# Attention by two pairs of heads at a time, and the order tables that go with it

## The chip, the cores and the metric

The kernel runs on one core of one Trainium2 chip. The metric is device time in microseconds (us) of one execution, lower is better. Engines are named as in the profile: PE (TensorE matmuls) and PEld (its weight loads), DVE (VectorE), ACT (ScalarE), POOL (GpSimd) and SP (SyncE, which issues most of the loads).

## What is computed

Two decoder layers over 256 tokens of width 1024. Layer 0 mixes tokens by a gated MLP, layer 1 by causal attention of 12 heads of 64; beside either stands a 4-head cross-attention into 256 memory tokens, and behind it an output projection, a LayerNorm of `alpha*x + sub`, a SwiGLU of inner width 2816 and another LayerNorm. Cut to what matters here:

```python
for i in range(2):
    if i == 0:
        u, v, q_mem = jnp.split(x @ a_w_in, ...)
        # gelu, LayerNorm of v; per group g: u * (tril(w_s[g]) @ v + b_s[g])
        mix = gmlp_mixer(u, v, ...)
    else:
        q, k, v, q_mem = jnp.split(x @ b_w_in, ...)
        # 12 heads of 64; the sequence is one block, so this is plain causal attention
        mix = moba_attention(q, k, v)
    mem_out = memory_cross_attention(q_mem, mem, w_mem_kv[i])     # 4 heads
    sub = jnp.concatenate([mix, mem_out], axis=-1) @ w_mix_out[i]
    x = layer_norm(ALPHA * x + sub, ...)
    x = layer_norm(ALPHA * x + swiglu(x, w_ffn_in[i], w_ffn_out[i]), ...)
```

## The kernel before, in words

Nearly every product is made from operands split into a high and a low part (`split`, L378: ACT rounds the high part, DVE subtracts it to get the low one), with three passes: high by high, low by high, high by low. Weights stream from memory in units of up to 1 MB (SP issues them, four buffers), and each half unit is split by ACT and DVE into one of ten buffers ahead of PE's use (`Stream`). PSUM holds eight tiles of 128 by 512: four with the tag acc (`acc_tile`, L382) and four with the tag mm (`mm_tile`, L385). A tile's bank comes free when its last reader is done.

**What sets the order.** PE executes its instructions in the order in which `build` writes them. DVE, ACT and SP execute theirs in the order of three tables (L293, L324, L349): number n is the n-th instruction that `build` gives to that engine, and `keep_order` (L358) forces the sequence. All engines run in order, so an instruction that waits holds back whatever its table places behind it. POOL has no table; it computes the reciprocal roots of the normalisations, masks the position weights wsT, and adds some weight blocks by DMA.

**Layer 0 around the change (L943 to L995).** On PE follow each other: the u projections (pu), the memory keys (hkm, from `mem_k`), the position products (sv, L968), the first half of the memory values (pvm, `mem_v`, L620), the memory scores (sm, `mem_scores`, L585), the second half of the memory values, and the output projection (opa). The position products multiply vn (the normalised v, made by DVE) as a 128-row, 64-column operand by wsT, three tiles of two groups of channels each. DVE then adds the bias (the third tile's bias is a load of its own, `in_bs`), multiplies by u, and splits the outcome into the mix tiles that the output projection reads.

**Layer 1's attention (L1041 to L1126).** Heads go in pairs, hp = 0 to 5. For one pair:

- `qk_half(hp, j)` (L1044): the projection to queries (j = 0) or keys (j = 1), 16 matmuls of the full array (qk in the profile); the result is split into the tile qks.
- `scores(hp)` (L1054): 12 matmuls that contract over 64 rows, the pair's two heads in the two halves of the array's rows (s), followed by a `Softmax` for each head (L557): DVE adds the mask and finds the row's extreme in a narrow (128) and a wide (256) part, ACT takes the two exponentials with their sums (z), and `normalise` on DVE takes the reciprocal and multiplies the two parts.
- `att_t(hp)` (L1063): six transposes (pt), copied to pT by ACT.
- `att_pv(hp)` (L1074): the value products, eight matmuls into 64 columns, one half of the columns for each head (pv); ACT and DVE split the result into mix[hp].

The memory attention of layer 1 does the same with its own scores (sm), transposes (ptm, `mem_transposes`, L597) and value products (pvm, `mem_pv`, L610, also 64 columns). In the old loop over i, pair i's projection halves alternate with the transposes of pair i-2, the scores of pair i-1 and the value products of pair i-2; every score group and nearly every value group stands alone between full-width products. The second halves of the projections use acc tiles, the first halves mm tiles.

The output projection (`OutProj`, L687) adds one term of six matmuls for each mix tile k and each of two token tiles tt (`step`, opc in the profile); `close` ends a token tile with its last two terms, followed by the LayerNorm's sums on DVE, the reciprocal root on POOL, the offset on DVE (ofc) and the scaling of two halves on ACT (L525). Then PE transposes the token tile (ptc, L531) for the FFN.

Of the kernel before, what the change touches and what calls it, by code (L numbers as in the profile page):

```python
# [21 lines left out]
P = 128  # L22
D = 1024
T = 256
# [169 lines left out]
class Stream:  # L194
# [128 lines left out]
)  # L323
SCALAR_ORDER = (  # L324
# [23 lines left out]
)  # L348
SYNC_ORDER = (  # L349
# [5 lines left out]
)  # L355


def keep_order(nc, tc, engine, order):  # L358

    mine = [i for i in nc.cur_bb.bb.instructions if i.engine == engine and not str(i.opcode).startswith("Tile")]  # L360
    assert len(mine) == len(order), (engine, len(mine))
    for a, b in zip(order, order[1:]):
        tc.add_manual_dep(mine[b], mine[a].name, mybir.DependencyInfo(
# [3 lines left out]
def build(nc, tc, ins, out):  # L367
    ET = mybir.EngineType
    with (
# [714 lines left out]
        for i in range(6):  # L1084
# [4 lines left out]
            if i >= 2:  # L1089
                pTs[i - 2] = att_t(i - 2)  # L1090
# [121 lines left out]
```

## Time and profile before

| what | value |
|---|---|
| median of 3 runs | 556.6 us (555.95 to 556.95) |
| the profiled execution's own time | 555.88 us |
| its span, first to last instruction | 554.1 us |
| mean granted TensorE clock | 0.997 |
| PE busy | 545.3 us, 98% of the span |
| PEld busy | 459.0 us, 83% |
| DVE busy | 501.9 us, 91% |
| ACT busy | 372.5 us, 67% |
| POOL busy | 49.5 us, 9% |
| moved by DMA | 120.97 MB, mean 218 GB/s |

The profile is of one execution. Rows of the chain of waits read "start, length, engine, tile, source line, count": the chain is followed back from the last instruction to whatever released each step. All matmuls carry L404, the line of a helper, so tiles tell them apart; 's' are scores, 'pv' value products, 'sv' position products. Rows of a timeline add the operation, the operands and, in brackets, how long the engine stood idle before and who ended that. A timeline's durations overlap a little from one instruction to the next. Rows of the stages give, for a stretch of time, the busy time and number of instructions of PE, PEld, DVE, ACT and POOL, the granted clock, the DMA share and GB/s.

### The profile page before, as it was taken

The numbers are of one execution on the slowest core, as the hardware profiler recorded it, in microseconds if no ns is written. First come the engines' busy times: TensorE is split into PE (matmuls) and PEld (weight loads), VectorE is DVE, ScalarE is ACT, GpSimd is POOL, SyncE is SP. The second block draws the span as 40 slices with busy tenths as digits, with TensorE's granted clock in tenths as the row PEclk, the third lists the DMA queues.
The fourth block names the chain that finished last, engine by engine and source line by source line (L and its number), as shares of the span: only waits on it lengthen the run. The fifth ranks groups of instructions, "written<-read, shape, count | busy, mean of one in ns | idle before, by whom it ended". The sixth has DMA issues, their size and how long they took to land.

```text
span 554.1 us, 7689 instructions
## 1 busy us (share of the span) xinstructions
PE 545.3 (98%) x2835; PEld 459.0 (83%) x2835; DVE 501.9 (91%) x707; ACT 372.5 (67%) x573; POOL 49.5 (9%) x59
## 2 busy tenths in 40 slices
PE   8999999999999999999999999999999999999994
PEld 8988878888888888888898888788888888888884
DVE  4799968999999999999989876578999999999997
ACT  4777768776768777773656767568767786877540
POOL 1002003020202010100100000101202020201001
PEclk9999999999999999999999999999999999999998
DMA  8997289467897788787368441172598798897622
GB/s 291 390 401 268 91 318 281 153 100 227 235 331 173 228 281 246 249 287 271 118 246 340 158 161 72 26 249 105 89 302 179 248 271 287 228 271 216 189 78 76
DMA packets 23718, 120.97 MB, mean 218 GB/s; under 512 B 2688, under 2 KB 4736, under 8 KB 13824
## 3 DMA queue, kind: packets, MB, share of 16 engines
q1 hardware_dynamic: 17344, 99.16, 47.5%
q0 software_dynamic: 5760, 20.97, 21.2%
q10 hardware_dynamic: 576, 0.34, 0.3%
q8 instruction: 22, 0.36, 0.3%
q14 instruction: 16, 0.13, 0.1%
HBM read 119.42 MB, written 1.05 MB: 217 GB/s over the span
## 4 chain that ended last, share of the span: by engine, by line
PE 96%; DMA 2%; SPq 1%; DVE 1%; issue 0%; ACT 0%; DVEq 0%
PE fof L404 11%; PE Xg L404 10%; PE Xf L404 10%; PE fog L404 9%; PE Zf L404 7%; PE Zg L404 7%; PE qk L404 6%; PE opc L404 4%; PE opa L404 4%; PE bv L404 3%; PE pu L404 3%; PE pvm L404 3%; PE hkm L404 2%; PE hqm L404 2%; PE pg L404 2%; PE pf L404 2%
## 5 line engine op out<-in xcount | busy, mean ns | idle before, releaser
L379 ACT CAST spl_s_M<-raw_s_T 128x1024 fp32r<-128x1024 f32 x80 | 82.8, 1053 | 35.9 <-DVE raw_s_T L259 32.1
L380 DVE TENSOR_TENSOR spl_s_M<-raw_s_T,spl_s_M 128x1024 fp32r<-128x1024 f32 x80 | 96.4, 1219 | 1.7 <-ACT spl_s_M L379 1.5
L379 ACT CAST spl_s_M<-raw_s 128x1024 fp32r<-128x1024 f32 x60 | 61.1, 1052 | 18.8 <-DMA raw_s<-in_w 13.9
L380 DVE TENSOR_TENSOR spl_s_M<-raw_s,spl_s_M 128x1024 fp32r<-128x1024 f32 x60 | 72.1, 1219 | 0.9 <-ACT spl_s_M L379 0.8
L404 PE MATMUL fof<-spl_w,htf 128*128 128x512 f32 x264 | 63.0, 390 | 0.0
L404 PEld LDWEIGHTS fof<-spl_w,htf 128*128 128x128 f32 x264 | 49.3, 188 | 10.2
L404 PE MATMUL fog<-spl_w,htg 128*128 128x512 f32 x228 | 54.2, 390 | 0.0
L380 DVE TENSOR_TENSOR spl_w<-raw_w,spl_w 128x1024 fp32r<-128x1024 f32 x44 | 53.1, 1219 | 0.8 <-ACT spl_w L379 0.8
L404 PEld LDWEIGHTS fog<-spl_w,htg 128*128 128x128 f32 x228 | 42.7, 188 | 8.8
L259 DVE TENSOR_TENSOR raw_s_T<-raw_s_T,raw_s 128x1024 f32<-128x1024 f32 x40 | 48.6, 1219 | 0.3
L379 ACT CAST spl_w<-raw_w 128x1024 fp32r<-128x1024 f32 x44 | 45.3, 1053 | 0.0
L220 POOL DMA_DIRECT2D raw_s<-in_w x20 | 17.2, 858 | 222.8 <-DVE spl_s_M L380 164.8
L404 PE MATMUL qk<-x2T,spl_qk 128*128 128x512 f32 x192 | 36.6, 344 | 0.0
L404 PEld LDWEIGHTS qk<-x2T,spl_qk 128*128 128x128 f32 x192 | 29.3, 188 | 5.2 <-issue 0.6
L404 PE MATMUL Xf<-spl_s_M,SfM 128*128 128x512 f32 x120 | 29.4, 393 | 0.0
L404 PE MATMUL Xg<-spl_s_M,SgM 128*128 128x512 f32 x120 | 29.3, 393 | 0.0
L404 PE MATMUL Xg<-spl_s_M,x3T 128*128 128x512 f32 x120 | 29.1, 390 | 0.0
L404 PE MATMUL Xf<-spl_s_M,x1T 128*128 128x512 f32 x120 | 29.0, 390 | 0.0
L404 PE MATMUL Zf<-spl_s_M,SfM 128*128 128x512 f32 x120 | 28.9, 389 | 0.0
L404 PE MATMUL Zg<-spl_s_M,SgM 128*128 128x512 f32 x120 | 28.8, 389 | 0.0
L404 PEld LDWEIGHTS Xg<-spl_s_M,x3T 128*128 128x128 f32 x120 | 22.4, 188 | 5.2 <-DVE x3T L380 0.4
L404 PEld LDWEIGHTS Xf<-spl_s_M,x1T 128*128 128x128 f32 x120 | 22.4, 188 | 4.9 <-DVE m5f L805 0.3
(264 smaller groups left out, 1070.5 us busy)
## 6 DMA issues: line engine op xcount, KB each, us to landing
raw_w<-in_w SPq DMA_DIRECT2D x22, 1024.0 KB, 6.9
raw_s<-in_w SPq DMA_DIRECT2D x20, 1024.0 KB, 7.0
raw_s_T<-in_w SPq DMA_DIRECT2D x10, 1024.0 KB, 6.0
raw_s_T<-in_w POOLq DMA_DIRECT2D x20, 512.0 KB, 7.9
raw_s<-in_w POOLq DMA_DIRECT2D x20, 512.0 KB, 5.6
raw_o<-in_w SPq DMA_DIRECT2D x8, 1024.0 KB, 7.2
raw_qk<-in_w SPq DMA_DIRECT2D x6, 1024.0 KB, 4.8
raw_v<-in_w SPq DMA_DIRECT2D x7, 512.0 KB, 8.7
```

What stands on the lines that cost most here:

```text
L220: self.nc.gpsimd.dma_start(self.raw[name][:, sl], self.unit_ap(other)[:, sl], accum_op=ALU.add)
L259: self.nc.vector.tensor_add(raw, raw, self.raw[used[1]][:, sl])
L379: nc.scalar.copy(hi, src)
L380: nc.vector.tensor_sub(lo, src, hi.bitcast(F32))
L404: nc.tensor.matmul(o, lhsT, rhs, start=start, stop=stop, skip_group_check=on)
```

## The change

The work is the same; its order changes. In layer 0 the first half of the memory values goes ahead of the position products, which so come directly before the memory scores. In layer 1 the loop over single pairs is written out for groups of two pairs: `pair_scores` makes the scores of two pairs and normalises their four softmaxes, `values` makes the value products of two pairs directly ahead of the next group's scores, and the memory value products (`mem_pv`) stand directly ahead of the scores of pairs 0 and 1. Both projection halves now use mm tiles, scores take acc tiles except those of pair 5, which take mm tiles. At the end, the output terms 0, 1 and 2 of token tile 0 stand in one run, the transposes of pairs 4 and 5 follow each other, and the term (1, 7) stands ahead of the closing of token tile 0. The three order tables are new throughout. Cut to its core:

```diff
@@ SCALAR_ORDER (start)
-    2, 0, 3, 4, 5, 6, 7, 9, 8, 11, 12, 10, 13, 14, 15, 17, 18, 16, 19, 26, 22, 27, 1, 24, 20, 31, 23, 32, 25, 41, 42,
+    2, 3, 4, 5, 6, 7, 8, 9, 11, 10, 13, 14, 12, 15, 16, 0, 17, 1, 18, 19, 26, 27, 22, 24, 25, 31, 20, 32, 23, 41, 21,
...
@@ SYNC_ORDER (start)
-    0, 1, 2, 3, 4, 18, 5, 6, 7, 8, 9, 11, 10, 12, 13, 14, 19, 20, 16, 21, 15, 17, 24, 25, 23, 22, 26, 27, 28, 29, 32,
+    0, 1, 2, 3, 4, 18, 5, 6, 7, 8, 10, 9, 11, 12, 13, 14, 15, 19, 20, 16, 17, 24, 22, 25, 21, 26, 27, 28, 29, 23, 31,
...
@@ layer 0
+        vm_part = mem_v("vm0", memx)
+        vm = vm_part(0)
         for jj in range(3):
             sv = acc_tile(f"sv{jj}").rearrange("p (j c t) -> p j c t", j=2, c=2)
...
-        vm_part = mem_v("vm0", memx)
-        vm = vm_part(0)
         nc.scalar.preload_act_table(AF.Exp)
         pr = mem_scores(qm, km, "m0", (acc_tile, acc_tile, mm_tile, mm_tile))
...
@@ layer 1
         def qk_half(hp, j):
-            t = (acc_tile if j else mm_tile)(f"qk{hp}{j}")
+            t = mm_tile(f"qk{hp}{j}")
...
-        def scores(hp):
+        def scores(hp, tile):
             st = qks[hp]
-            ss = [acc_tile(f"s{hp}{par}") for par in range(2)]
+            ss = [tile(f"s{hp}{par}") for par in range(2)]
...
+        def pair_scores(hps, tiles):
+            for n, hp in enumerate(hps):
+                prs[hp] = scores(hp, tiles[n])
+            for hp in hps:
+                for p in prs[hp]:
+                    p.normalise()
+
+        def values(hps):
+            for hp in hps:
+                att_pv(hp)
+
+        qk_half(0, 0)
+        pr_mem = mem_scores(qm, km1, "m1", (acc_tile, acc_tile, mm_tile, mm_tile))
+        qk_half(0, 1)
...
+        for p in pr_mem:
+            p.normalise()
+        qk_half(1, 0)
+        pts = mem_transposes(pr_mem, "1", (0, 1))
+        qk_half(1, 1)
+        pts += mem_transposes(pr_mem, "1", (2, 3))
+        qk_half(2, 0)
+        mem_pv(pts, vm1, mix, "1")
+        pair_scores((0, 1), (acc_tile, acc_tile))
+        qk_half(2, 1)
+        qk_half(3, 0)
+        pTs[0] = att_t(0)
+        qk_half(3, 1)
+        pTs[1] = att_t(1)
+        qk_half(4, 0)
+        values((0, 1))
+        pair_scores((2, 3), (acc_tile, acc_tile))
+        qk_half(4, 1)
+        qk_half(5, 0)
+        pTs[2] = att_t(2)
+        qk_half(5, 1)
+        pTs[3] = att_t(3)
         op = OutProj(1, mix, "c")
         op.step(0, [6, 7], first=True)
+        values((2, 3))
+        pair_scores((4, 5), (acc_tile, mm_tile))
+        op.step(0, [0, 1, 2])
         pTs[4] = att_t(4)
-        prs[5] = scores(5)
-        for p in prs[5]:
-            p.normalise()
-        op.step(0, [0])
-        att_pv(4)
-        op.step(0, [1])
         pTs[5] = att_t(5)
-        op.step(0, [2])
-        att_pv(5)
+        op.step(0, [3])
         op.step(1, [6], first=True)
-        op.step(0, [3])
+        values((4, 5))
+        op.step(1, [7])
         op.close(0, [4, 5], xres)
-        op.step(1, [7, 0, 1, 2, 3])
+        op.step(1, [0, 1, 2, 3])
```

Read through `build`, the table entries that the prediction speaks of mean this. On ACT, 10 and 12 are the copies of the fifth and sixth x0T (0 is the first table load, 17 the last value cast). On SP, 29 is the load of raw_km1 and 23 that of the third bias. On DVE, the softmaxes of pairs 4 and 5 stand at the places 447 to 468 of the new table, with the low halves of mix 2 and 3 among them, and in front of them the two halves of the first FFN weight and the last three steps of qks5.

More of the change, by code (lines that the diff above doesn't have):

```diff
@@ L1081, in att_pv @@
             split(mix[hp][:, 0, :], mix[hp][:, 1, :], o[:, :256])
-        pts = []
-        for i in range(6):
-            qk_half(i, 0)
-            if i in (1, 2):
-                for p in pr_mem[2 * i - 2:2 * i]:
-                    p.normalise()
-            if i >= 2:
-                pTs[i - 2] = att_t(i - 2)
-            if i >= 1:
-                prs[i - 1] = scores(i - 1)
-                for p in prs[i - 1]:
-                    p.normalise()
-            if i == 0:
-                pr_mem = mem_scores(qm, km1, "m1", (acc_tile, acc_tile, mm_tile, mm_tile))
-            qk_half(i, 1)
-            if i == 0:
-                mix += [actp.tile([P, 2, T], F32R, tag=f"mix{k}", name=f"mix1_{k}") for k in range(6, KT)]
-            if i >= 2:
-                att_pv(i - 2)
-            if i in (1, 2):
-                pts += mem_transposes(pr_mem, "1", (2 * i - 2, 2 * i - 1))
-            if i == 3:
-                mem_pv(pts, vm1, mix, "1")
+        def pair_scores(hps, tiles):
[3 more added lines that the diff above has]
+                for p in prs[hp]:
+                    p.normalise()
@@ new lines, in values @@
+        def values(hps):
[4 more added lines that the diff above has]
+        qk_half(0, 1)
+        mix += [actp.tile([P, 2, T], F32R, tag=f"mix{k}", name=f"mix1_{k}") for k in range(6, KT)]
+        for p in pr_mem:
[4 more added lines that the diff above has]
+        pts += mem_transposes(pr_mem, "1", (2, 3))
@@ L1108, in build @@
+        pair_scores((4, 5), (acc_tile, mm_tile))
+        op.step(0, [0, 1, 2])
         pTs[4] = att_t(4)
-        prs[5] = scores(5)
-        for p in prs[5]:
-            p.normalise()
-        op.step(0, [0])
-        att_pv(4)
-        op.step(0, [1])
         pTs[5] = att_t(5)
-        op.step(0, [2])
-        att_pv(5)
+        op.step(0, [3])
         op.step(1, [6], first=True)
-        op.step(0, [3])
+        values((4, 5))
+        op.step(1, [7])
         op.close(0, [4, 5], xres)
-        op.step(1, [7, 0, 1, 2, 3])
+        op.step(1, [0, 1, 2, 3])
```

110 rows, old and new, of tables (SCALAR_ORDER, SYNC_ORDER, VECTOR_ORDER) are left out of this document.

## The prediction

> **What bounds the kernel now.** I read the page first, then the busy time by stage, then the chain of waits in order of time, then the timelines of DVE and ACT around the attention of layer 1.
>
> ```profile
> span 554.1 us, 7689 instructions
> ...
> PE 96%; DMA 2%; SPq 1%; DVE 1%; issue 0%; ACT 0%; DVEq 0%
> ```
>
> The chain that ends last is PE for 96% of the span. So a microsecond counts only if PE's own sequence gets shorter, or if PE is made to wait. The next view gives busy time by stage (columns PE, PEld, DVE, ACT, POOL, clock, DMA share, GB/s).
>
> ```profile
> 51.00:61.50 10.50, 10.50 (x106) 9.24 (x106) 10.50 (x20) 7.41 (x14) 0.00 (x0) 1.00 0.42 130
> 298.43:370.34 71.91, 71.91 (x474) 58.53 (x475) 53.37 (x157) 47.93 (x120) 2.30 (x3) 1.00 0.44 148
> 447.00:478.00 31.00, 31.00 (x143) 25.70 (x142) 29.90 (x30) 22.48 (x27) 4.29 (x5) 1.00 0.89 263
> ```
>
> PE has no gap in any of them. In the attention stretch (second row) DVE has 18.5 us to spare and ACT 24, so small additions there hide. In layer 0's gating (first row) DVE has nothing to spare: what comes late there comes late for good. In the FFN (third row) the change moves nothing but orders, and I cost that at nothing: the DVE fills 29.9 of 31.0 us and follows PE, which releases its buffers; were that cover gone, each microsecond of DVE delay would show as one.
>
> A PE that is always busy can still lose time, and the chain shows where (start, length, what):
>
> ```profile
> 51.04 2.77 PE sv L404 x48
> 53.81 3.03 PE pvm L404 x16
> ...
> 61.47 6.83 PE opa L404 x30
> ...
> 71.44 1.88 PE pvm L404 x16
> ...
> 306.79 3.02 PE qk L404 x16
> ...
> 310.67 2.78 PE qk L404 x16
> ...
> 327.21 0.81 PE pv L404 x8
> 328.01 1.73 PE pvm L404 x16
> 329.74 3.03 PE qk L404 x16
> ...
> 357.83 12.51 PE opc L404 x54
> ```
>
> The same 16 products of a projection half take 2.78 us behind transposes (310.67), but 3.02 behind scores (306.79) and 3.03 behind value products (329.74). The memory value products take 1.88 behind full-width products and 1.73 straight behind pv, which has their shape (128 rows by 64 columns). So each passage between the full array and a part of it costs something, and products of one shape side by side pay nothing between them. **Prices:** leaving scores 3.02-2.78 = 0.24; leaving value products 0.25; entering value products 1.88-1.73 = 0.15. Entering scores has no row of its own: bounds are 0 and 0.24, the price of leaving them, and I take 0.15, the entry of the other part shape. One visit to scores then costs 0.39, one to values 0.40.
>
> **The change part by part.**
>
> *Visits in layer 1.* The scores of the memory attention keep their place. Besides them the old order makes six visits for scores and six for values (pv1 and pvm stand together): 6 x 0.39 + 6 x 0.40 = 4.74 us. The new one makes four: pvm with scores 0 and 1, values 0 and 1 with scores 2 and 3, values 2 and 3 with scores 4 and 5, values 4 and 5 alone. Three of them enter as values and leave as scores (0.15 + 0.24), one is of values (0.40): 1.57 us, and three boundaries inside, from 128x64 values to 64x128 scores, which no row shows. Below, such a boundary could cost 0, as between pv and pvm; above, all of a leaving and an entering, 0.40. I take 0.2, because both sides are parts but not the same part, and the nearest row, an entry of 0.15, is a change of shape too. Saved: 4.74 - 1.57 - 0.6 = 2.57 (1.97 to 3.17).
>
> [...]
>
> *The visit in layer 0.* The position products (sv) now stand directly before the memory scores, and the first half of the memory values, a full-width product, goes ahead of them. Two visits (0.40 + 0.39) become one with a boundary inside (0.15 + 0.24 + 0.2): 0.2 saved (0 to 0.4, by the boundary's bounds). All else on PE is the same products in another order.
>
> *The start.* The new ACT table puts the fifth x0T copy ahead of the sixth, and moves the first table load (it ran while ACT waited for data) in front of the last value cast.
>
> ```profile
> 13.81 0.71 ACT L439 CAST x0T<-raw_v 128x256 fp32r<-128x256 f32 x2 [0.43 <-DMA raw_v<-in_w]
> ```
>
> ACT waited 0.43 us for the sixth copy's data with the fifth queued behind it, and PE's products of the fifth step began after it. I credit 0.2 (0 to 0.43). The table load is hidden by the four steps of products that PE still has ahead of it there; without that cover its whole length would show.
>
> *Softmaxes four at a time.* This is what the change adds as a wait. Behind scores 4 and 5 PE has only the terms 0, 1, 2 of the output projection, 18 x 0.23 = 4.1 us (54 products in 12.51 above; a term is six), where two softmaxes stood before and four stand now. On ACT and DVE one softmax is made of these (the second fence is DVE):
>
> ```profile
> 352.28 0.51 ACT L576 ACTIVATE pb<-pb,mb 128x256 f32<-128x256 f32 x1 [0.34 <-DVE mb L567]
> 352.69 0.19 ACT L576 ACTIVATION_READ_ACCUMULATOR pb<-pb,mb 128x1 f32 x1
> 352.79 0.39 ACT L576 ACTIVATE pb<-pb,mb 128x128 f32<-128x128 f32 x1
> ...
> 353.67 0.35 ACT L379 CAST mix<-pv 128x256 fp32r<-128x256 f32 x1
> ...
> 368.91 0.81 ACT L525 ACTIVATE xres<-xres,ofc,rsc 128x512 f32<-128x512 f32 x1
> ```
>
> ```profile
> 350.62 0.42 DVE L380 TENSOR_TENSOR mix<-pv,mix 128x256 fp32r<-128x256 f32 x1 [2.59 <-ACT mix L379]
> ...
> 353.79 0.17 DVE L580 RECIPROCAL zb<-zb 128x2 f32<-128x2 f32 x1
> 353.99 0.55 DVE L582 TENSOR_SCALAR pb<-pb,zb 128x256 f32<-128x256 f32 x2
> ...
> 366.17 0.16 DVE L523 SCALAR_TENSOR_TENSOR ofc<-mvc,rsc 128x1 f32<-128x1 f32 x1 [0.74 <-POOL rsc L522]
> ```
>
> A wide exponential holds ACT for 0.51, a narrow one for 0.39, and a mix copy takes 0.35; neighbours overlap by 0.09 or so (352.69 + 0.19 against 352.79). Count from the first output term after the scores. Scores 4 end about one score earlier, so ACT's first exponential can begin at -0.3 (estimate). In the new ACT table the wide one of pair 4's second head is the seventh entry: three narrow, two wide and two mix copies, 2.9 less 0.2 of overlap, end at 2.4. DVE then has a reciprocal (0.17), two normalisings (0.55 the pair) and the low half of pair 2's values (0.42), 1.1: done at 3.5. PE wants that half a third into its third term, at 0.1 + 14 x 0.23 = 3.3. I reckon 0.2 us of waiting here. By the same count DVE's last normalising ends at 5.1, and its transposes stand at 5.0: 0.1. Before all this, score 5 starts as DVE finishes the last low half of qks5, which now stands behind two weight halves: 0.2. The earlier groups have two projection halves, 5.8 us, before their first transposes and four softmaxes are 4 x 0.9 on ACT, so nothing. Together 0.5 (0 to 1.5).
>
> *Ends that move closer.* The term (1, 7) moves ahead of the closing of tile 0, so that 24 products instead of 30 cover tile 0's normalisation. That closing now ends 24 products into the last 54, at 357.8 + 24 x 0.23 = 363.4, and the offset is there at 366.3 (the 366.17 row): 2.9 us, plus two scalings of 0.81 (the 368.91 row): 4.5, under 24 x 0.23 = 5.5. The new ACT table lets both scalings follow each other, where a weight cast stood between them. Nothing, with 1.0 in hand; were it gone, each microsecond would show. The j=1 halves move from the acc to the mm banks: their readers are done before the next tile asks, except for score 5, counted above. The memory softmaxes are normalised before the second projection group instead of across two: DVE has the slack.
>
> *Position products later.* sv needs both normalised vn halves, and memory value half 0 gives DVE 3.0 us more for them, of which the new DVE table spends most on output weights put ahead. I take 0.15 of waiting (0 to 0.8).
>
> **Sum:** 2.57 + 0.2 + 0.2 - 0.5 - 0.15 = 2.3 us. Against the profiled execution, 555.88 us (span 554.1 and 1.8 around it), this gives 553.6; that execution lies 0.7 under the median of the runs, 556.6, so the median to expect is 554.3. Not all bounds are met at once; with the boundary at either end and half of the others the case runs from 553.2 to 555.7.
>
> **The rivals.**
>
> *More is saved.* The boundary inside a visit costs nothing: 4 x 0.2 more, 553.5. For it: pv and pvm. Against it: the shapes differ here.
>
> *The softmaxes come late everywhere.* Each of the three groups in layer 1 waits about 0.6 more than reckoned, 1.7 together: 556.0, no change that can be told (0.2%, 1.1 us, is about what a measurement of this kernel can tell). For it: ACT and DVE are in fixed order, and casts that wait for weight buffers stand among the exponentials. Against it: DVE's slack.
>
> *Nothing is saved.* The price hangs on each group of products and not on the passage: 2.77 less, 557.1, within what can't be told. Against it: 1.73 beside 1.88.
>
> *Slower, through a bias.* The load of the third group's bias moves, in SP's queue, behind a weight load that waits for a free buffer.
>
> ```profile
> raw_km<-in_w SPq DMA_DIRECT2D x1, 1024.0 KB, 5.0
> ...
> vn<-in_bs SPq DMA_DIRECT2D x1, 128.0 KB, 10.0
> ```
>
> ```profile
> 51.54 0.33 SPq L241 DMA_DIRECT2D raw_km<-in_w  x1
> ```
>
> If that weight load is issued at 51.5 as before, the bias follows at 52 and lands behind its 5.0 us, at 57, just when the third bias add wants it (sv ends at 51.04 + 3.03 + 2.77 = 56.8 now). If it takes 10.0 us as before, it lands at 62, and DVE, in order, holds the mix halves, the memory softmaxes and the second half of output weight 0 behind that add. By my count of the new DVE table that weight half is split one microsecond before PE wants it for its second output term (61.5 + 1.4 = 62.9); 5 us later on DVE are 4.0 lost on PE: 558.3. It turns to a loss from a landing at about 60.3. Against it: the 10.0 was with other loads ahead of it, and around 52 the core moves only 130 GB/s (first row of the stages).
>
> **How the numbers follow.** Forecast 0.60, more saved 0.10, late softmaxes 0.18, nothing saved 0.03, the bias 0.09. The first two are faster: 0.70; the next two about the same: 0.21; the last slower: 0.09. The range is the forecast's own, opened downward for a cheaper boundary and a better start at once, and upward for the late softmaxes: 552.9 to 556.4.
>
> **What would show it.** In the chain after: projection halves at 3.0 us only behind scores, three in the main stretch and not ten; scores in pieces of about 1.6 for two pairs; values in pieces of 1.5; output terms without a break. Wrong on the boundary: a pair of scores behind values beginning with no gap, or with 0.4. Wrong on the softmaxes: PE waiting at the third output term, or before pt, for DVE. Wrong on the bias: gt's third add idle on a DMA. PE starting earlier than 14.58 would confirm the start; a wait at sv, the last term.

## The result and the profile after

| | before | after | ratio, 95% interval |
|---|---|---|---|
| first comparison, medians of 5 runs | 556.6 us (555.68 to 556.95) | 552.6 us (552.34 to 553.36) | 0.9933 [0.9919, 0.9948] |
| second comparison (run a2 below) | 555.89 us (11 runs) | 552.72 us (5 runs) | 0.9948 [0.9936, 0.9960] |
| the profiled execution | 555.88 us, span 554.1 | 552.48 us, span 550.8 | |

The change is faster by 3.7 us (2.9 to 4.5) in the first comparison and by 2.9 us (2.2 to 3.6) in the second. The prediction was 554.3 us, with a range from 552.9 on. The direction was right, the size was not: 552.6 lies just below that range.

From the page of the kernel after (span; PE's row; the shares of the chain that ended last):

```profile
span 550.8 us, 7698 instructions
...
PE 542.6 (99%) x2835; PEld 460.6 (84%) x2835; DVE 501.5 (91%) x707; ACT 374.5 (68%) x574; POOL 47.7 (9%) x59
...
PE 98%; DMA 1%; DVE 1%; DVEq 0%; ACT 0%; issue 0%
```

PE still sets the end, with 2.7 us less of its own time than the 545.3 of before. The stages, in the columns of the prediction's table (layer 0's gating, and the attention from the memory scores to the first transposes for the FFN):

```profile
50.57:60.79 10.22, 10.22 (x105) 9.01 (x105) 10.11 (x19) 7.68 (x14) 1.00 (x1) 1.00 0.51 171
297.13:367.20 70.07, 70.07 (x475) 58.82 (x475) 52.36 (x156) 47.11 (x121) 3.15 (x3) 1.00 0.40 134
```

The attention takes 70.07 us where it took 71.91. The chain of waits of the kernel after (start, length, engine, tile, line, count), layer 0 first, then the value projection's end, then the attention:

```profile
50.57 2.77 PE pvm L404 x16
53.34 2.77 PE sv L404 x48
...
60.79 6.81 PE opa L404 x30
...
278.57 0.87 PE ptb L531 x8
279.45 9.36 PE bv L404 x54
...
313.83 1.58 PE s L404 x24
315.41 5.85 PE qk L404 x32
...
328.21 1.50 PE pv L404 x16
329.71 1.58 PE s L404 x24
...
344.05 1.50 PE pv L404 x16
345.55 1.77 PE s L404 x20
347.32 4.55 PE opc L404 x18
351.87 1.31 PE pt L1068 x12
...
357.45 9.75 PE opc L404 x42
367.20 0.87 PE ptc L531 x8
...
370.81 2.72 PE Xg L404 x12
```

Values and scores of two pairs stand side by side (1.50 and 1.58, 329.71 begins where 328.21 ends), and projections come in runs of 32 with one costly exit (5.85, twice 2.78 and 0.29). Two things are longer than they need be: the last scores (1.77 where the others take 1.58) and the output terms behind them (4.55). One thing is shorter whose code the change left alone: the last row, the first products of the second FFN. In the kernel before it is

```profile
373.95 3.02 PE Xg L404 x12
```

To see where the time went I lay the start times of the same marks beside each other, in the executions that were profiled. What does not depend on the kernel's stage falls out as a spread. "Old" and "new" say which code and orders the stage had in that kernel; each number is the difference of two start times in a chain of waits, the last one of the span's end and a start.

| stage | old (us) | new (us) | saved |
|---|---|---|---|
| start to the first hqm | 23.30, 22.75, 22.63, 24.70, 22.80 | 22.83, 22.85, 23.46, 23.34, 22.87 | not shown |
| hqm to opa (layer 0) | 38.17, 38.19, 38.18, 38.17 | 37.96, 37.92, 37.93, 37.93 | 0.24 |
| Xf to ptb (first FFN) | 168.47, 168.32, 168.33, 168.73 | 168.29, 168.29, 168.30, 168.30 | 0.17 (0.02 to 0.44) |
| ptb to hqm (value projection) | 21.57, 21.57, 21.57, 21.57 | 21.17, 21.17, 21.16, 21.17 | 0.40 |
| hqm to Zg (attention and its end) | 101.39, 101.38 | 99.24, 99.28, 99.26 | 2.13 |
| of that, ptc to Zg (behind the attention) | 21.16, 21.15 | 20.85, 20.84, 20.88, 20.84 | 0.30 |
| Zg to the end | 162.60, 162.64, 162.68 | 162.75, 162.77, 162.74 | -0.11 |

The stages that repeat make 2.8 us. The pair of executions first compared differs by 3.3, and 0.47 of that is the start, 23.30 against 22.83, which the other executions do not confirm. (Run a2 of the kernel after is left out of the first two rows: its first loads landed late, its chain goes through them and reaches opa only at 62.04. Left out of rows too, and told below, are s1, layer 0 of s2, the attention of e3b and of f1 to f3, and the ends of e3b and f2. d0 to d3, which have the new first orders too, began hqm at 22.55 to 23.10.)

### The profile page after: what moved, and what is told of

It reads as the page before. It is cut to its first block, busy times and chain, and to the rows that moved or that the text cites. A ratio compares the mean times of both kernels' runs of the same rounds, so it can differ in the third digit from the quotient of the medians.

```text
span 550.8 us, 7698 instructions
## 1 busy us (share of the span) xinstructions
PE 542.6 (99%) x2835; PEld 460.6 (84%) x2835; DVE 501.5 (91%) x707; ACT 374.5 (68%) x574; POOL 47.7 (9%) x59
## 3 DMA queue, kind: packets, MB, share of 16 engines
HBM read 119.42 MB, written 1.05 MB: 219 GB/s over the span
## 4 chain that ended last, share of the span: by engine, by line
PE 98%; DMA 1%; DVE 1%; DVEq 0%; ACT 0%; issue 0%
PE fof L404 11%; PE Xf L404 10%; PE Xg L404 10%; PE fog L404 9%; PE Zg L404 7%; PE Zf L404 7%; PE qk L404 6%; PE opc L404 4%; PE opa L404 4%; PE va L404 3%; PE bv L404 3%; PE pu L404 3%; PE pvm L404 3%; PE hkm L404 2%; PE hqm L404 2%; PE pg L404 2%
## 5 line engine op out<-in xcount | busy, mean ns | idle before, releaser
L404 PEld LDWEIGHTS Zg<-spl_s_M,SgM 128*128 128x128 f32 x120 | 22.5, 188 | 4.8 <-DVE SgM L380 0.2
```

Of the source, the lines that this page charges most:

```text
L404: nc.tensor.matmul(o, lhsT, rhs, start=start, stop=stop, skip_group_check=on)
```

## The experiments

In e1 to e4, and in s1 and s2, the tables are put together from pieces of the old and the new ones, cut where both have issued the same instructions; `old` and `new` stand for the instructions, which are renumbered for the code in use.

**e1: the attention alone.** Layer 1's code is the new one, with new orders inside the attention only.

```diff
-VECTOR_ORDER = old
+VECTOR_ORDER = old[:345] + new[345:480] + old[480:]
-SCALAR_ORDER = old
+SCALAR_ORDER = old[:276] + new[276:372] + old[372:]
```

> Only layer 1's attention is changed (its code, and the orders of the engines from its memory query to its output projection); the value products of layer 0 and all other orders are those of before. Theory A (the gain is made of three parts: the attention by two pairs, the start and layer 0, and the small waits that the other stages' orders take away): the chain from hqm of layer 1 to ptc is 1.8 us shorter than before's 74.7, everything else is as before, and the time is 1.8 under before, about 554.8. Theory B (the attention alone carries the gain): 4.0 under before, about 552.6. Theory C (the orders elsewhere carry it, the regrouping is taken back by its own waits): within 0.5 of before.

Measured: 555.51 us (11 runs), 0.9993 [0.9984, 1.0003]. None of the three theories has it: theory C has the size (0.4 under before, by the ratio) but not the reason, since what took the gain back stands behind the attention and not in it. Up to the last value products the attention ran as in the kernel after; then its chain left PE:

```profile
356.60 1.50 PE pv L406 x16
358.10 2.96 PE opc L406 x12
...
366.82 1.03 ACT spl_r_A L381
367.86 0.49 ACT xres L527
368.47 1.99 ACT spl_r_B L381 x2
...
372.55 3.31 PE Xg L406 x12
```

The old order on ACT puts a cast of a weight half (spl_r_A, 366.82) between the two scalings of the normalised rows (xres), and two more (spl_r_B) ahead of the copies that Xg reads. In the old code 30 products covered the normalisation, in the new code 24 do, and Xg comes late and takes 3.31. From hqm to Zg e1 takes 100.94, so of 2.13 only 0.45 is kept. Of the 1.8 that the shorter sequence is worth up to ptc in the kernel after, three quarters were lost again while the order behind it was made for the longer one.

**e4: the attention with the new orders behind it.**

```diff
-VECTOR_ORDER = old
+VECTOR_ORDER = old[:345] + new[345:]
-SCALAR_ORDER = old
+SCALAR_ORDER = old[:276] + new[276:]
-SYNC_ORDER = old
+SYNC_ORDER = old[:72] + new[72:]
```

> The attention's new code with the new orders from the attention to the end of the kernel; the start, layer 0 and the orders up to the memory query are those of before. Run e1 kept 0.45 us of the attention's gain up to Zg, since with the old orders behind it the chain went through the layer norm. Theory A: with its own end orders the stretch from hqm to Zg takes 99.2 as in the kernel after, 2.15 shorter than before's 101.4, with no other difference: about 554.0. Theory B (the end orders need the other new orders too): over 100 again.

Measured: 554.09 us (10 runs), 0.9963 [0.9952, 0.9975], which is 2.1 us (1.4 to 2.7); hqm to Zg 99.28. Theory A. The regrouping and the orders behind it are worth 2.1 together. The regrouping alone is worth 0.45 (e1); what the orders bring alone, e3b shows.

**e3b: orders without new code.** TensorE's program is that of before throughout. (e3, a first form of it, has no time: its entries for layer 0 carried the numbers of the new code, and its engines waited for one another in a circle.)

```diff
-VECTOR_ORDER = old
+VECTOR_ORDER = old[:111] + new[111:345] + old[345:480] + new[480:]
-SCALAR_ORDER = old
+SCALAR_ORDER = old[:110] + new[110:276] + old[276:372] + new[372:]
-SYNC_ORDER = old
+SYNC_ORDER = old[:41] + new[41:72] + old[72:84] + new[84:]
```

> TensorE's program, the start, layer 0 and the attention are those of before; only the orders of VectorE, ScalarE and the load queue between layer 0's output projection and layer 1's attention, and from the last mix and output terms on, are the new ones. Theory A (orders by themselves are worth something where they end a wait): the stretch from ptb to hqm is 0.4 us shorter, as in the kernel after, and ptc to Zg 0.3 shorter, 0.7 in all. Theory B (orders follow the timing of the code that they were made for): ptb to hqm is 0.4 shorter, since TensorE's program is the same there, but behind the old attention the new end orders make the layer norm or the first FFN products wait, and ptc to Zg gets no shorter or longer.

Measured: 555.76 us (10 runs), 0.9994 [0.9983, 1.0005]. By stage: ptb to hqm 21.17, so the 0.40 came with the orders alone. ptc to Zg takes 20.84 against 21.16: the end orders bring 0.3 behind the old attention too, as theory A has it. Yet hqm to Zg takes 101.45 against 101.39, since 0.38 was lost ahead of ptc. Rows of its chain:

```profile
297.17 1.15 PE sm L406 x14
298.35 0.74 PE sm L406 x8
...
373.07 2.72 PE Xg L406 x12
```

Xg takes 2.72 where it took 3.02. The memory scores come in two pieces and take 1.92 where before's take 1.63; the second piece needs a low half of qqm from DVE, right where the new table ends and the old one goes on (that PE waits for it is an estimate from the tables, no row names it), and the first scores behind them lose the other 0.09. So theory A holds by its stages, and the seam of the splice hides half of it in the time. (Its profiled execution also lost 0.6 behind Zg, see the last section.) The 0.40 can be read directly. These are the rows of DVE in the kernel before (start, length, line, operation, operands, idle time and who ended it), and PE's rows there:

```profile
278.31 1.42 DVE L512 SCALAR_TENSOR_TENSOR xres<-xres,rsf,gb0ffn 128x512 f32<-128x512 f32 x2 [0.44 <-POOL rsf L508]
279.64 0.95 DVE L380 TENSOR_TENSOR spl_bv<-raw_bv,spl_bv 128x768 fp32r<-128x768 f32 x1
```

```profile
279.48 1.02 PE ptb L531 x8
280.50 9.61 PE bv L404 x54
```

DVE waits 0.44 for POOL, then scales, and only then makes the last weight half of the value projection (279.64); its end, at 280.59, is where PE's bv can go on. PE's last transposes wait for the second half of that scaling (1.02 for 0.87). The new table puts the weight half ahead of the scaling, DVE no longer waits for POOL there, and the rows become 0.87 and 9.36.

**e2: the start and layer 0 alone.** Layer 0's code is the new one.

```diff
-VECTOR_ORDER = old
+VECTOR_ORDER = new[:111] + old[111:]
-SCALAR_ORDER = old
+SCALAR_ORDER = new[:110] + old[110:]
-SYNC_ORDER = old
+SYNC_ORDER = new[:41] + old[41:]
```

> Only the start and layer 0 are changed: the position products stand before the memory scores, and the orders of the engines up to the end of layer 0's output projection are the new ones; from there on all is as before. Theory A: hqm starts 0.47 earlier, opa 0.7 earlier in all, and this is kept to the end, since TensorE is never off the chain: about 555.9. Theory B: what is gained here is waited away at the first later stage whose loads or weight halves come no earlier, within 0.2 of before.

Measured: 555.28 us (11 runs), 0.9989 [0.9980, 0.9998], 0.6 us (0.1 to 1.1). From hqm to opa 37.92, kept to the end. Theory A on layer 0; the start (22.85) says nothing, as e1 and e3b, with the old first entries, began hqm at 22.75 and 22.63.

**s1 and s2: the first entries alone, both ways.** s1 is the kernel before with new first entries, s2 the kernel after with old ones.

```diff
-VECTOR_ORDER = old
+VECTOR_ORDER = new[:18] + old[18:]
-SCALAR_ORDER = old
+SCALAR_ORDER = new[:30] + old[30:]
-SYNC_ORDER = old
+SYNC_ORDER = new[:30] + old[30:]
```

> The kernel before with the new first entries of the three tables alone (18 of VectorE's, 30 of ScalarE's, 30 of the load queue's). Theory A (the 0.47 us by which the two profiled executions differ at the first hqm is the orders' doing): 0.47 under before, about 555.6 beside 556.1, and hqm starts at 22.8. Theory B (it is the spread of the first loads' landing: with the old first entries hqm started at 23.30, 22.75, 22.63 and 24.70, with the new ones at 22.55 to 23.46): the interval of the ratio holds 1, and hqm starts anywhere between 22.5 and 23.5.

> The opposite: the kernel after with the old first entries of the three tables. Theory A: 0.47 over the kernel after, about 553.1, hqm at 23.3. Theory B: as the kernel after, about 552.6 to 552.9, hqm anywhere between 22.5 and 24.7; from hqm on every stage as in the kernel after (opa 37.95 behind hqm, ptb 168.3 behind Xf, hqm of layer 1 21.17 behind ptb, Zg 99.2 behind that).

Measured: s1 566.34 us, 1.0199 [1.0179, 1.0219]; s2 553.79 us, 0.9966 [0.9954, 0.9978], both against before. Neither theory held in s1. The chain of s1, and its longest wait of PE (in total, times, longest):

```profile
30.45 13.06 DMA mraw<-in_memT
```

```profile
PE pu L406 <- DVE uT L953: 7.0, 1, 7.0
```

A load of the memory now lands late, ACT holds its copy of it in front of uT, and PE waits 7.0 us. Behind that wait PE is slow for a while: the next 48 products of pu take 9.90, where half of the 16.64 that 96 take elsewhere would be 8.32, and the four runs of s1 have a mean granted clock of 0.986 to 0.991, the ten of before beside them 0.995 to 0.997. In s2 hqm started at 22.80 with the old first entries (theory B), but opa came 39.07 behind it and not 37.95: theory B's second half failed. The chain of s2 there runs through DVE's weight halves and memory copies; DVE, with next to no slack in layer 0 (10.50 us of 10.50 in the prediction's row), got behind. So the first entries of the three tables belong to the rest of layer 0, and a price for "the start orders" by themselves cannot be taken from a splice. Whether the new ones start PE earlier stays open.

**d0 to d3: the price of a visit by itself.** Sixteen times, behind each step of layer 1's value projection in the kernel after, stand four products whose result is not read, in one execution of each kernel: full width (d0), 64 rows as in scores (d1), 64 columns as in values (d2), columns and then rows (d3).

```diff
+                dr = [mm_tile(f"dr{tt}{k}{par}") for par in range(2)]
+                for n in range(2):
+                    for par in range(2):
+                        mm(dr[par][:, :256], x2T[rows(par), k, 0, :P], w[rows(par), 0, :256], n == 0, n == 1)
```

> The kernel after with extra work in the value projection of layer 1: behind each of its 16 steps stand four more products of 128 rows by 128 columns of the array, 256 wide, whose result is not read. Baseline for the next three. Theory A: 16 times four products at about 0.11 us, and nothing at the way in or out: the stretch from ptb to hqm, 21.2 in the kernel after, takes about 28.2.

> As d0, but each group of four extra products is of 64 rows by 128 columns, two and two beside each other as in the scores. Theory A (each visit to a group of such products costs 0.39 us whatever surrounds it): the two pairs take about 0.22 and the visit 0.39: about 21.2 + 16 * 0.61 = 31.0, longer than d0 although half as much array time is used. Rival (the price is in waits of the scores for their softmaxes or tiles, not in the visit): 21.2 + 16 * 0.22 = 24.7.

> As d0, but each group of four extra products is of 128 rows by 64 columns in full precision, as in the value products. The extra group's own time is read from the spacing of its products in the trace (0.6 to 0.75 by the value products' rows). Theory A: 0.40 us more than that for each visit. Rival: nothing more.

> As d0, but with the group of d2 and, right behind it, the group of d1. Theory A (a boundary from values to scores costs 0.2, as the kernel after shows it twice): each step costs d1's and d2's extra together less 0.2, so the stretch is 16 * 0.2 = 3.2 shorter than d1 and d2 together add. Rivals: the boundary is free (6.3 shorter), or it costs as much as leaving and coming in (no shorter).

One step of each, from the chains of d0, d1, d2 and d3 (the six products of the projection and the extra group; the four calls of the value shape, in full precision, stand as eight in the trace):

```profile
274.10 0.47 PE du L404 x4
274.57 1.05 PE bv L404 x6
```

```profile
272.36 0.43 PE dr L404 x4
272.80 1.25 PE bv L404 x6
```

```profile
272.02 1.02 PE dc L404 x8
273.05 1.25 PE bv L404 x6
```

```profile
272.41 1.02 PE dc L404 x8
273.43 0.43 PE dr L404 x4
273.86 1.25 PE bv L404 x6
```

The same six products take 1.05 us behind full-width ones and 1.25 behind either part shape. Measured from the FFN's last products to hqm, the stretch takes 20.29 in the kernel after, and 27.98, 30.29, 39.68 and 46.71 in d0 to d3: 0.48, 0.62, 1.21 and 1.65 a step. Four full products cost 0.48, so two pairs of them 0.24, and a visit to scores costs 0.62 - 0.24 = 0.38. Eight of the value shape take 0.865 with nothing around them, by the sixteen in 1.73 straight behind pv (328.01 in the prediction), so a visit to values costs 1.21 - 0.865 = 0.35. d3 is 0.62 + 1.21 - 1.65 = 0.18 cheaper than d1 and d2 together: what falls away is one leaving (1.25 against 1.05), while the four dr take 0.43 behind dc as they do behind full-width products, so the boundary between the two shapes still costs an entering, about 0.2. Theory A in all four, d2's visit a little cheaper than it said: half the array's work (d1) takes longer than the whole of it (d0).

These rows show a price at each change of shape, 0.38 and 0.35 for a visit and about 0.2 between the two part shapes; what makes it they do not show.

**f1: the two waits taken away.** In the kernel after, DVE makes the last low half of qks5 behind two weight halves, and PE's second scores wait for it; DVE's low half of mix 2 holds the third output term. Its rows there:

```profile
343.97 1.21 DVE L380 TENSOR_TENSOR spl_s_M<-raw_s_T,spl_s_M 128x1024 fp32r<-128x1024 f32 x1
...
345.90 0.41 DVE L477 SCALAR_TENSOR_TENSOR qks<-qk,qks 128x256 fp32r<-128x256 f32 x1
...
350.21 0.42 DVE L380 TENSOR_TENSOR mix<-pv,mix 128x256 fp32r<-128x256 f32 x1
```

f1 reorders VectorE only (d = spl_s_M's two halves, q = qks5's four steps, m2 and m3 = the low halves of mixes 2 and 3, r and n = the softmaxes' reductions and scalings, m4 = the low half of mix 4).

```diff
-d1 q0 d0 q1 q2 q3   r4 r5   n4 m2 n4 n5 m3 n5   m4
+d1 q0 q1 q2 q3   r4 r5   m2 n4 n5 m3   d0 m4
```

> The kernel after, with VectorE's order changed around the last pair of heads alone: the four steps of the last pair's queries and keys stand before the second weight half of the first FFN block, which moves behind the softmaxes, and the low half of the third pair's output stands before the scaling of the softmaxes. Theory A: the second scores piece of the last group goes from 1.77 to 1.58 and the output piece behind it from 4.55 to 4.32, and the time falls by 0.4, to about 552.2. Rival: the transposes of the last pairs are late next, as the softmaxes end no earlier than before: 0.2 of it comes back as a wait ahead of them, 552.4.

Measured: 552.85 us, 0.9942 [0.9930, 0.9955]. Its chain:

```profile
346.15 1.58 PE s L406 x24
347.73 4.33 PE opc L406 x18
352.06 1.54 PE pt L1070 x12
```

Scores 1.77 to 1.58, output terms 4.55 to 4.33, as theory A has it; then the transposes 1.31 to 1.54, as the rival has it: 0.19 + 0.22 - 0.23 = 0.18 saved (hqm to Zg 99.05). In the time this is not told apart from the kernel after.

**f2 and f3: the wait that followed.** One fourth output term between the two pairs' transposes, and ScalarE's table load ahead of the last pair's copies, on top of f1. The two are one kernel; f3 ran beside the kernel after.

```diff
         pTs[4] = att_t(4)
-        pTs[5] = att_t(5)
         op.step(0, [3])
+        pTs[5] = att_t(5)
```

> As f1 (the last pair's queries and keys before the weight half, the third pair's low half before the scalings), and TensorE takes the fourth output term between the transposes of the last two pairs, with ScalarE's table load ahead of the last pair's copies. Theory A: the 0.23 us that f1 gave back at the transposes (1.54 for twelve in place of 1.31) is gone, two transposes of 0.66 stand apart at no price, and the stretch from hqm to Zg is 0.4 under the kernel after's 99.24: 98.8. Rival: the last pair's values wait for the copies of the transposes that now come 1.4 later: a wait of 0.2 to 0.5 ahead of them, 99.0 to 99.3.

> The kernel of f2 again, on the same chip and against the same runs of before as the kernel after. Theory A: the 0.34 us that its stretch from hqm to Zg is shorter shows in the time, 0.3 under the kernel after. Theory B: it is taken back behind Zg (f2's profiled execution lost 0.6 in the second FFN, where weight halves came late), no difference.

Measured: f2 552.99 us, 0.9939 [0.9922, 0.9955]; f3 552.17 us, 0.9940 [0.9928, 0.9952]. The chain of f3:

```profile
347.14 4.33 PE opc L406 x18
351.47 0.66 PE pt L1070 x6
352.12 1.47 PE opc L406 x6
353.60 0.66 PE pt L1070 x6
```

Both halves of the transposes take 0.66, no wait is left but 0.08 in the fourth term, and hqm to Zg is 98.90 and 98.92, near theory A's 98.8. In this stage it beats the kernel after by 0.35; the times on one chip, 552.17 and 552.72, lie in that order, but their ratios' intervals overlap, so f3 is faster than before and not told apart from after.

**a2: the kernel after again.**

> The kernel after, unchanged, beside many runs of before on one chip. The stages located so far (layer 0, the FFN's small waits, the value projection, the attention) make 2.8 us; the first comparison measured 4.0 by medians of five runs each. Theory A (the first five runs of before stood high by chance): 3.0 to 3.4 under before, ratio 0.994 to 0.9946. Theory B (something that the profiled executions don't show is saved too): 4.0 again, ratio 0.993 or less.

Measured: 552.72 us against 555.89, 0.9948 [0.9936, 0.9960]. The medians differ by 3.2, the ratio says 2.9 (2.2 to 3.6): theory A, with the lower edge of theory A's band passed by a little. In four comparisons with 10 to 23 runs each, the median of before was 556.11, 555.80, 555.85 and 555.89; the 556.6 known at the prediction stood 0.7 above them, and the profiled execution's 555.88 among them.

## Why the prediction was wrong, point by point

**What bounds the kernel** held: PE is 98% of the chain after, and every saving that was found is one of PE's own time or of a wait of PE.

**The prices of a visit** held, measured by themselves: 0.38 and 0.35 against 0.39 and 0.40, a boundary at about 0.2 against 0.2. The rival in which the boundary is free and the one in which the price hangs on groups both fall with d1 to d3.

**The visits' sum** was 2.57. From qk to ptc the chains give 74.68 and 72.84, 1.84 saved, and the two waits that f1 takes away cost 0.19 + 0.22, so the visits brought 2.25. Part of the missing 0.3 lies where visits end: I took 0.24 or 0.25 for leaving, but before's exit from values towards transposes cost only 0.15 (1.02 against 0.87, at 318.81), and two of the remaining exits behind scores (5.85 less twice 2.78) cost 0.29. The rest I have not traced. The sum is inside the bounds given.

**Softmaxes four at a time:** 0.2 for score 5 (0.19 measured), 0.2 at the third output term (0.22), and 0.1 at the last transposes, which did not show in the kernel after and came as 0.23 once the others were gone. The estimate was right in kind and nearly in size.

**Layer 0:** 0.2 was forecast for the visit, 0.24 measured. The 0.15 of waiting at sv did not come: sv takes 2.77 at 53.34, as it did before. The bias rival did not come about either; its load was issued as reckoned, at 51.56, and took 4.8 us:

```profile
51.56 0.42 SPq L934 DMA_DIRECT2D vn<-in_bs  x1
```

```profile
vn<-in_bs SPq DMA_DIRECT2D x1, 128.0 KB, 4.8
```

**The start:** 0.2 was credited, and PE starting earlier than 14.58 named as its sign. The sign was worthless: with the old first entries e1's value projection runs in one piece from 5.19. One execution's stall was taken for the order's.

**The steps that failed** are two.

First, "in the FFN the change moves nothing but orders, and I cost that at nothing", and the like "nothing" for the ends that move closer. I asked only whether a new order could delay PE, and never what the old order was already costing it. The value projection's 0.40 could be read in the trace of before: eight transposes in 1.02 us that take 0.87 elsewhere, and a weight half behind a scaling that waits for POOL. So could the 0.30 behind the attention, where twelve products of Xg take 3.02, and 2.73 when they come next (394.67). The first FFN gave another 0.17, the stretch behind Zg took back 0.11: in all some 0.76 for a term put at nothing. On the ends the prediction was right that the new order on ACT was needed for them to cost nothing: with the old one e1 gave back 1.4 of its 1.8.

Second, the step from the profiled execution to the median. The sum gave 553.6 against the profiled 555.88; I added 0.7, since that execution lay under the median of three runs, and came to 554.3. The four later medians, on four chips, say that the execution was typical and the three runs were high; how many microseconds are saved does not hang on it. Of the 1.7 between 554.3 and 552.6 it is the largest piece, 0.7; 0.5 is what the stages saved beyond the sum (2.8 against 2.3), and the rest is open. The sum came as near as it did partly by luck: without the start and the sv wait, which the runs do not confirm, 2.57 + 0.2 - 0.5 = 2.27 was forecast for the two places with visits, and they gave 1.83 + 0.24 = 2.07, while the orders, put at nothing, gave 0.76.

What stays open: between 555.88 less 2.8, 553.1, and the medians of 552.6 and 552.7 are another 0.4 to 0.5. A shorter start on average, which ten executions cannot separate from their spread of 22.6 to 24.7, would explain it; so would chance, as the second comparison's interval reaches from 2.2 to 3.6.

## What to carry to other kernels

On an engine that is never idle, count its passages between the full array and a part of it, price them from equal pieces behind different neighbours, and check what is late next at each place where the sequence gets shorter. A new order is never costed at nothing: look in the stage for pieces that are longer than their twins elsewhere, since a wait that already stands there can go, and for casts placed ahead of a step that the shorter cover no longer hides. Set the sum against several medians, and don't correct it by the distance of one execution from three runs.

## What the runs showed of the hardware that was not expected

- In e4 and in the kernel after the first value products went at two paces, the slow one for different lengths of time. In e4 the first 24 value products took 6.32 us, in the kernel after the first 35 took 6.95. Rows of PE's timeline, e4 and then after:

```profile
5.90 6.32 PE L406 MATMUL va<-spl_v,x0T 128*128 128x384 f32 x24 [0.72 <-DVE x0T L442]
```

```profile
5.31 6.95 PE L404 MATMUL va<-spl_v,x0T 128*128 128x384 f32 x35
```

In after two of them are spaced at 0.320 us and later ones at 0.174. By the two rows e4 has some nine more at the slow pace (an estimate: 6.95 less eleven at 0.174 is 5.04 for 24, and the 1.28 from there to 6.32 is 8.8 times the 0.146 between the paces). e4's hqm starts at 24.70, after's at 22.83; the nine are 1.3 of this 1.9, and e4's first product, 0.6 later, is the rest. From 6 to 12 us the stages give the granted clock as 1.00 in both all the same, but the trace's first record of it begins, in after, only where the pace changes, at 6.64; in before it begins at 4.26, and the value products there, from 5.37 on, have none at the slow pace. What sets how long the slow pace lasts, these traces do not show.

- Two executions, of e3b and f2, took 163.3 us from Zg to the end where ten others, with the same orders or the old ones, took 162.60 to 162.77. In e3b three groups of the second FFN took 2.85 to 2.91 in place of 2.72; its chain stays on PE there and names no cause. f3, the same kernel as f2, did not show it. In f2 the chain goes through two loads of raw_s, of 7.71 and 8.98 us, and the cast behind the second starts at 454.51, 66.3 behind Zg; in after, whose chain stays on PE there, that cast starts at 453.13, 65.1 behind Zg. So in f2 a weight that landed late is the likely cause of the half microsecond, which, as f3 shows, does not belong to the kernel.
